# Weight sums of a seven-product scheme formed from DRAM to DRAM by GpSimd's DMAs, and the last down products in five groups between the pairs

## Chip, core and metric

One core of one Trainium2 chip runs one program. The metric is the device time of one execution in microseconds; lower is better. The kernel before takes 2364.74 us, the median of three runs (2363.32 to 2365.43).

## What is computed

Two transformer blocks run one after the other, in 32-bit floating point. The first block has two layers over 16 meta tokens and 512 tokens, width 1024. The second block, which the change touches, has one layer over 512 tokens: a mixer of four branches, then a gated feed-forward of width 2816. Its last part is

```python
h = rms_norm(x, ffn_norm)
act = jax.nn.silu(h @ w_gate) * (h @ w_up)
x = x + act @ w_down          # w_gate, w_up: 1024 x 2816, w_down: 2816 x 1024
```

## The kernel before, in words

**Layout.** Everything is held transposed: `hT` is eight tiles of 128 features by 528 positions in SBUF. A weight tile (128 x 1024, 512 KB) holds the 128 output features of one step for all eight blocks of input features.

**Precision.** Each 32-bit matrix is split into a high part (`hi`, a cast by ScalarE, now and then by VectorE) and a low part (`lo`, a subtraction on VectorE). A product is three matmuls for each block: high by high, high by low, low by high. So each weight goes through a raw place, a high place and a low place in SBUF.

**Order of the work.** A helper class `Order` (from line 382) records every operation; `flush` (line 505) plans them at the end of each stage, with modelled costs (`cost`, line 413), delays between engines (`latency`, line 368), and a rank for each stage (`RANK`, line 362), in which the record number stands against the length of the chain of work that still follows. Stage 5 of six, `block2_mixer` (line 1336), has rank (1, 30); the last, `block2_ffn` (line 1728), has (1, 5). `flush` fixes only the order of the instructions on each engine's own queue. The engines run by themselves and wait for each other by semaphores where data or places demand it. All operations are issued by one line of a helper, L493, so the profile names that line for nearly everything, and the tiles tell the groups apart. All DMAs are issued by SyncE's queue (SP). GpSimd (POOL) sets four constants at the start and does nothing else.

**The last stage.** Output tiles f = 0 and 1 of gate and up are plain products: 24 matmuls of 512 columns each (`gate_up`, line 1843). For f = 2 to 21, gate and up are computed together as one two by two block product by seven products in place of eight (`gate_up_fast`, line 1815; called a pair here): 7 x 4 x 3 = 84 matmuls of 256 columns. It needs sums of weight blocks. `weights` (line 1801) loads two packed rows `r1` and `r2` of `w_gs2` and forms `s13` (1024 columns, one addition on VectorE) and `s24` (two additions of 512 columns), then splits `r1`, `s13`, `s24` and half of `r2` into high and low. The raw, high and low places are rings of five tiles each (line 1747): three that the whole kernel uses (`w_raw`, `w_hi`, `w_lo`) and two of this stage (`s_raw`, `s_hi`, `s_lo`).

The down product (`down`, line 1853) goes by groups of f, (0, 8), (8, 16) and (16, 22) (`GROUPS`, line 29). For each of the eight output tiles m it loads one weight tile, splits it, multiplies, and VectorE adds the result into `hT[m]`. A group's down product is recorded behind the first pair of the next group; the last one, with the stores of the output, ends the kernel. `early` (line 1750) moves the records of loads and splits ahead by 500 numbers, so that they are planned before the products they serve.

Of the kernel before, what the change touches and what calls it, by code (L numbers as in the profile page):

```python
# [11 lines left out]
F32 = mybir.dt.float32  # L12
F32R = mybir.dt.float32r
AF = mybir.ActivationFunctionType
ALU = mybir.AluOpType
AX = mybir.AxisListType
PSUM = bass.MemoryType.PSUM
DRAM = bass.MemoryType.DRAM

P = 128  # L20
D = 1024
KD = 8
# [4 lines left out]
DFF = 2816  # L27
NFT = DFF // P
GROUPS = ((0, 8), (8, 16), (16, 22))
EPS = 1e-6  # L30
NEG = -(2.0 ** 100)
FILL = -3.0e38
# [11 lines left out]
FS = 2  # L44
# [145 lines left out]
def prepare(i):  # L190
    i = {k: np.asarray(v) for k, v in i.items()}
    a = {}
    a["h0"] = np.concatenate([i["meta_tokens"], i["x"][0]], 0).T.reshape(KD, P, NR)
    a["w_even"] = pack(i["even_w_in"][0], even_tiles())
    wo = i["even_w_out"][0]
    a["w_eo_0"] = pack(wo[512:512 + RF * P], whole(0, D))
    a["w_eo_1"] = pack(np.concatenate([wo[512 + RF * P:], wo[:512]], 0), whole(0, D))
    for l in range(2):
        g, u = pack(i["ffn_w_gate"][l], whole(0, DFF)), pack(i["ffn_w_up"][l], whole(0, DFF))
        a[f"w_gu{l}"] = np.stack([g, u], 1).reshape(2 * NFT, P, D)  # L200
        for n, (f0, f1) in enumerate(GROUPS):
            a[f"w_dn{l}_{n}"] = pack(i["ffn_w_down"][l][f0 * P:f1 * P], whole(0, D))
    a["w_odd"] = pack(i["odd_w_in"][0], odd_tiles())
    oo = i["odd_w_out"][0]
    a["w_oo_0"] = pack(oo[:OSP * P], whole(0, D))
    a["w_oo_1"] = pack(oo[OSP * P:], whole(0, D))
    a["w_2"] = pack(i["w_in_2"][0], list(w2_list().values()))
    for n, k in enumerate(("w_fox_out_2", "w_conv_out_2", "w_mlstm_out_2", "w_swa_out_2")):
        a[f"w_br{n}"] = pack(i[k][0], whole(0, D))
    a["w_mg"] = pack(i["w_merge_out_2"][0], whole(0, D))  # L210
    g, u = pack(i["w_gate_2"][0], whole(0, DFF)), pack(i["w_up_2"][0], whole(0, DFF))
    a["w_gu2"] = np.stack([g[:FS], u[:FS]], 1).reshape(2 * FS, P, D)
    a["w_gs2"] = paired(g[FS:], u[FS:]).reshape(-1, P, D)
    for n, (f0, f1) in enumerate(GROUPS):
        a[f"w_dn2_{n}"] = pack(i["w_down_2"][0][f0 * P:f1 * P], whole(0, D))
    g = [col(i["norm_mix"][0]), col(i["norm_ffn"][0]), col(i["norm_mix"][1]), col(i["norm_ffn"][1]),
         col(i["norm_final"]), col(i["attn_norm_2"][0]), col(i["ffn_norm_2"][0]), col(i["even_gn_gain"][0])]
    a["gains"] = np.concatenate(g, 1)
    cw = [np.concatenate([col(i["ffn_conv_w"][l][t]) for t in range(3)] + [col(i["ffn_conv_b"][l])], 1) for l in range(2)]
    a["convp"] = np.concatenate(cw, 1)  # L220
    two = lambda v: np.concatenate([v, v])[:, None]
    a["hgain"] = np.concatenate([two(i["fox_q_gain_2"][0]), two(i["fox_k_gain_2"][0]), two(i["swa_q_gain_2"][0]),
                                 two(i["swa_k_gain_2"][0]), col(i["mlstm_h_gain_2"][0])]
                                + [col(i["conv_w_2"][0][t]) for t in range(3)], 1)
    a["hbias"] = np.stack([i["fox_f_bias_2"][0], i["mlstm_i_bias_2"][0], i["mlstm_f_bias_2"][0]], 1)
    a["sinks"] = i["swa_sinks_2"]
    a["rb1"] = i["rel_bias"]
    a["rb2"] = i["rel_bias_2"]
    a = {k: np.ascontiguousarray(v) for k, v in a.items()}
    a.update(constants())  # L230
    return a
# [134 lines left out]


def latency(a, b):
    return 2.1 if a == "SP" else LAT.get((a, b), 0.25)


class Engine:
# [9 lines left out]
class Order:  # L382
# [16 lines left out]
    def pool(self, es, name, bufs=1, space=None, side=None):  # L399
        kw = {} if space is None else {"space": space}  # L400
        if side is not None:
            kw["side"] = side
        if space is not DRAM:
            kw["reuse_waits"] = "tile"
        real = es.enter_context(self.tc.tile_pool(name=name, bufs=bufs, **kw))
        return Pool(self, real, bufs, space is PSUM, space is DRAM)
# [6 lines left out]
    def cost(self, eng, method, out, ins, k):  # L413
        n = max([self.size(out)] + [self.size(i) for i in ins if isinstance(i, View) and method in ("max", "tensor_reduce", "bn_stats")])
        if eng == "PE":
            if method == "transpose":
                return max(256, 2 * n) / 2400 + 0.003
            return (max(256, n) if ins[0].t.dt == F32R else max(512, 4 * n)) / 2400 + 0.003
        ps = any(isinstance(i, View) and i.t.pool.psum for i in ins) or out.t.pool.psum
        ptrs = sum(1 for i in ins if isinstance(i, View) and self.size(i) == 1 and n > 1)  # L420
        if eng == "ACT":
            return (0.051 if ps else 0.093) + n * 0.833e-3 + 0.093 * (ptrs + (k.get("accum_out") is not None))
        if eng == "DVE":
            c = 0.069 + 0.06 * min(ptrs, 1)
            if method == "reciprocal":
                return c + n * 6.0e-3
            if method in ("tensor_copy", "tensor_scalar") and not ps:
                return c + n * 0.521e-3
            return c + n * 1.042e-3
        if eng == "SP":  # L430
            nb = 4 * int(np.prod(out.shape))
            return max(0.1, nb / 332e3)
        return 0.1 + n * 2.2e-3

    def record(self, eng, method, a, k, also=()):
        out = a[0]
# [148 lines left out]
def body(ctx: ExitStack, tc, A, out):  # L585
# [3 lines left out]
    V, SC, G, T, DMA = O.V, O.A, O.G, O.T, O.D  # L589
    pool = lambda name, **k: O.pool(ctx, name, **k)  # L590

    def dma(o, i):
        DMA.dma_start(o, i)
# [16 lines left out]
            return (pd, pp, pd, pp, pd, pp, pp)[AllBanks.turn % 7].tile(shape, dt, name=("d", "at", "d", "at", "d", "at", "at")[AllBanks.turn % 7])  # L610

    pall = AllBanks()

    def const(name, shape, dt=F32, pl=None):
        t = (pl or cst).tile(shape, dt, name=name)
# [7 lines left out]
    for k in range(KD):  # L623
        t = res.tile([P, NR], F32, name=f"h{k}")
# [711 lines left out]
    def block2_mixer():  # L1336
        with ExitStack() as es:
# [3 lines left out]
            yp = P_("yp", bufs=1)  # L1341
            wk = P_("wk", bufs=1)
            unit = lambda name, bufs=1, p=P, dt=F32: wk.tile([p, S], dt, name=name, bufs=bufs)

            x = nxt_[0].x
            rc = rp.tile([P, 8], F32, name="rcol")
# [381 lines left out]
    def block2_ffn():  # L1728
        with ExitStack() as es:
# [20 lines left out]
            def early(fn):  # L1750
                O.shift -= 500
                v = fn()
                O.shift += 500
                return v

            def halves(raw, hi=None, lo=None):

                n = raw.shape[1]
                hi = his.tile()[:, :n] if hi is None else hi
                lo = los.tile()[:, :n] if lo is None else lo  # L1760
                SC.copy(hi, raw)
                V.tensor_tensor(lo, raw, hi.bitcast(F32), op=ALU.subtract)
                return v2(hi, P), v2(lo, P)

            def load(name, i, n=D):
                raw = raws.tile()[:, :n]
                dma(raw, A[name][i])
                return raw


# [30 lines left out]
            def weights(f):  # L1801


                r1, r2 = load("w_gs2", 2 * (f - FS)), load("w_gs2", 2 * (f - FS) + 1)
                s13, s24 = raws.tile(), raws.tile()
                two = lambda t: t.rearrange("p (a b) -> p a b", a=2)
                V.tensor_tensor(two(s13), two(r2)[:, 0:1, :].to_broadcast([P, 2, 512]), two(r1), op=ALU.add)
                V.tensor_tensor(s24[:, :512], s13[:, :512], r1[:, 512:], op=ALU.add)
                V.tensor_tensor(s24[:, 512:], s24[:, :512], r2[:, 512:], op=ALU.add)
                w1, w24, w13 = halves(r1), halves(s24), halves(s13)  # L1810
                a12 = halves(r2[:, 512:], *(fp.tile([P, 512], F32R, name=n, bufs=2) for n in ("s_hi2", "s_lo2")))
                part = lambda w, i: tuple(v[:, 4 * i:4 * i + 4, :] for v in w)
                return part(w1, 1), a12, part(w1, 0), part(w13, 0), part(w24, 0), part(w13, 1), part(w24, 1)

# [35 lines left out]
                proj(pall, wtile("w_gu2", 2 * f + 1), x, times(g, g), ONE)  # L1850
                acts[f] = split_new(g, fp, "ah", "al", 10, S)

            def down(gi):
                f0, f1 = GROUPS[gi]
                n = (f1 - f0) * P
                a = [acts[f][0] for f in range(f0, f1)], [acts[f][1] for f in range(f0, f1)]
                for m in range(KD):
                    w = early(lambda: halves(load(f"w_dn2_{gi}", m, n)))
                    proj(pall, w, a, add_h(m, NM), ONE)
                    if gi == 2:  # L1860
                        dma(out[P * m:P * m + P, :], hT[m][:, NM:])

            for gi, (f0, f1) in enumerate(GROUPS):
                for f in range(f0, f1):
                    gate_up(f)
                    if gi and f == f0:
                        down(gi - 1)
            down(2)
            O.flush()

    steps = [even_mixer, lambda: ffn(0, 1), odd_mixer, lambda: ffn(1, 3), block2_mixer, block2_ffn]
# [16 lines left out]
```

## Time and profile before

| | |
|---|---|
| median of three runs | 2364.74 us (2363.32 to 2365.43) |
| the profiled execution, its own time | 2365.07 us |
| its span, first to last instruction | 2362.9 us |
| mean granted TensorE clock | 0.998 |
| busy: TensorE (PE), its weight loads (PEld) | 2334.1 us (99%), 2125.5 us (90%) |
| busy: VectorE (DVE), ScalarE (ACT), GpSimd (POOL) | 1793.0 us (76%), 968.3 us (41%), 0.2 us |
| DMA moved | 205.98 MB, mean 87 GB/s |

Matmuls are pipelined, so the busy time of one overlaps that of the next and a busy PE is not one at its peak. Waits are put down to the instruction that ended them. In the table of stretches the columns are the stretch and its length, then busy time and number of instructions of each engine, the granted clock of TensorE as a share of full speed, the mean busy share of the 16 DMA engines, and the GB/s moved.

### The profile page before, as it was taken

The numbers are of one execution on the slowest core, as the hardware profiler recorded it, in microseconds if no ns is written. First come the engines' busy times: TensorE is split into PE (matmuls) and PEld (weight loads), VectorE is DVE, ScalarE is ACT, GpSimd is POOL, SyncE is SP. The second block draws the span as 40 slices with busy tenths as digits, with TensorE's granted clock in tenths as the row PEclk, the third lists the DMA queues.
The fourth block names the chain that finished last, engine by engine and source line by source line (L and its number), as shares of the span: only waits on it lengthen the run. The fifth ranks groups of instructions, "written<-read, shape, count | busy, mean of one in ns | idle before, by whom it ended". The sixth has DMA issues, their size and how long they took to land.

```text
span 2362.9 us, 38568 instructions
## 1 busy us (share of the span) xinstructions
PE 2334.1 (99%) x15488; PEld 2125.5 (90%) x15488; DVE 1793.0 (76%) x3512; ACT 968.3 (41%) x1842; POOL 0.2 (0%) x4
## 2 busy tenths in 40 slices
PE   7999999999999999999999999999999999999999
PEld 7999999999999999999888888877888888889998
DVE  6999898764655779997665647876898877987965
ACT  4423556310111278885211203344677613443422
POOL 0000000000000000000000000000000000000000
PEclk9999999999999999999999999999999999999999
DMA  5222221322222211103223223322222122332322
GB/s 200 70 72 70 73 84 57 111 92 90 90 90 88 93 64 55 55 25 102 90 90 100 90 90 97 122 70 86 82 90 72 53 95 89 102 122 80 126 77 84
DMA packets 66546, 205.98 MB, mean 87 GB/s; under 512 B 7972, under 2 KB 14576, under 8 KB 66368
## 3 DMA queue, kind: packets, MB, share of 16 engines
q1 hardware_dynamic: 66368, 203.53, 27.1%
q8 instruction: 121, 1.98, 0.4%
q14 instruction: 57, 0.47, 0.1%
HBM read 201.37 MB, written 6.84 MB: 88 GB/s over the span
## 4 chain that ended last, share of the span: by engine, by line
PE 94%; DVE 3%; DMA 2%; issue 1%; ACT 1%; SPq 0%; DVEq 0%; ACTq 0%
PE d L493 54%; PE at L493 37%; PE pv L493 2%; DMA w_raw<-w_even 1%; DVE w_lo L493 1%; DVE s_lo L493 1%; DVE w_raw L493 0%; DMA w_raw<-w_gs 0%; DVE g L493 0%; DMA h<-h 0%; ACT w_hi L493 0%; DMA ob<-c_oh 0%; DVE sqh L493 0%; DVE s_raw L493 0%; SPq L493 0%
## 5 line engine op out<-in xcount | busy, mean ns | idle before, releaser
L493 PE MATMUL d<-xh,w_hi 128*128 128x264 f32 (+5 forms) x2082 | 616.2, 318 | 8.1 <-ACT w_hi L493 8.0
L493 PE MATMUL d<-xl,w_hi 128*128 128x264 f32 (+5 forms) x2082 | 618.4, 319 | 1.1 <-DVE xl L493 1.0
L493 PE MATMUL d<-xh,w_lo 128*128 128x264 f32 (+5 forms) x2082 | 614.0, 318 | 0.0
L493 DVE TENSOR_TENSOR w_lo<-w_raw,w_hi 128x1024 fp32r<-128x1024 f32 (+4 forms) x363 | 401.1, 1107 | 53.2 <-PE d L493 18.4
L493 PEld LDWEIGHTS d<-xh,w_hi 128*128 128x128 f32 x2082 | 377.4, 189 | 36.3 <-ACT w_hi L493 8.0
L493 PEld LDWEIGHTS d<-xl,w_hi 128*128 128x128 f32 x2082 | 377.3, 189 | 25.9 <-DVE xl L493 2.3
L493 PEld LDWEIGHTS d<-xh,w_lo 128*128 128x128 f32 x2082 | 376.3, 189 | 26.6 <-issue 1.9
L493 ACT CAST w_hi<-w_raw 128x1024 fp32r<-128x1024 f32 (+5 forms) x181 | 172.8, 955 | 328.2 <-PE d L493 230.5
L493 DVE CAST w_hi<-w_raw 128x1024 fp32r<-128x1024 f32 (+4 forms) x182 | 116.4, 640 | 188.0 <-PE d L493 113.0
L493 PE MATMUL at<-xh,w_hi 128*128 128x264 f32 (+3 forms) x822 | 240.1, 302 | 1.2 <-DVE h L493 1.2
L493 PE MATMUL at<-xh,w_lo 128*128 128x264 f32 (+3 forms) x822 | 240.1, 302 | 0.0
L493 PE MATMUL at<-xl,w_hi 128*128 128x264 f32 (+3 forms) x822 | 240.1, 302 | 0.0
L493 ACT ACTIVATE y<-g,cp 128x528 f32<-128x528 f32 (+1 forms) x44 | 36.2, 824 | 345.6 <-DVE g L493 345.6
L493 PEld LDWEIGHTS at<-xh,w_hi 128*128 128x128 f32 x822 | 152.8, 189 | 7.5 <-issue 1.6
L493 PEld LDWEIGHTS at<-xh,w_lo 128*128 128x128 f32 x822 | 152.8, 189 | 5.4
L493 PEld LDWEIGHTS at<-xl,w_hi 128*128 128x128 f32 x822 | 152.6, 189 | 5.2
L493 PE MATMUL at<-ah,w_lo 128*128 128x264 f32 (+1 forms) x350 | 113.0, 331 | 0.0
L493 PE MATMUL at<-ah,w_hi 128*128 128x264 f32 (+1 forms) x350 | 113.0, 332 | 0.0
L493 PE MATMUL at<-al,w_hi 128*128 128x264 f32 (+1 forms) x350 | 112.9, 332 | 0.0
L493 PE MATMUL d<-ah,w_hi 128*128 128x264 f32 (+1 forms) x274 | 91.1, 333 | 0.0
L493 PE MATMUL d<-al,w_hi 128*128 128x264 f32 (+1 forms) x274 | 91.0, 332 | 0.0
L493 PE MATMUL d<-ah,w_lo 128*128 128x264 f32 (+1 forms) x274 | 90.7, 332 | 0.0
(604 smaller groups left out, 4849.9 us busy)
## 6 DMA issues: line engine op xcount, KB each, us to landing
w_raw<-w_gu SPq DMA_DIRECT2D x92, 512.0 KB, 3.7
w_raw<-w SPq DMA_DIRECT2D x59, 512.0 KB, 3.6
w_raw<-w_dn SPq DMA_DIRECT2D x42, 512.0 KB, 3.8
w_raw<-w_even SPq DMA_DIRECT2D x41, 512.0 KB, 3.8
w_raw<-w_gs SPq DMA_DIRECT2D x25, 512.0 KB, 3.6
w_raw<-w_odd SPq DMA_DIRECT2D x24, 512.0 KB, 3.5
w_raw<-w_dn SPq DMA_DIRECT2D x21, 384.0 KB, 3.1
s_raw<-w_gs SPq DMA_DIRECT2D x15, 512.0 KB, 3.6
```

The source lines that it names most:

```text
L493: return f(*[r(x) for x in a], **{n: r(x) for n, x in k.items()})
```

## The change

The sums `s13` and `s24` are no longer made by VectorE. At the place in the program where the mixer begins, five DMAs for each of the 20 pairs are recorded on GpSimd's queue. They copy blocks of the weights from DRAM into new DRAM tiles of the pool `far` and add other blocks to them as they are written. The last stage loads `s13` and `s24` like any weight, and only the needed half of `r2`. The down product goes in five groups, and its output tiles are spread over the pairs of the next group in place of standing behind its first pair. The planner's numbers for POOL change with it (no other operation runs there).

```diff
--- before.py
+++ after.py
@@ -27,6 +27,7 @@
 DFF = 2816
 NFT = DFF // P
 GROUPS = ((0, 8), (8, 16), (16, 22))
+GROUPS2 = ((0, 5), (5, 10), (10, 15), (15, 19), (19, 22))
 EPS = 1e-6
 NEG = -(2.0 ** 100)
 FILL = -3.0e38
@@ -211,7 +212,7 @@
     g, u = pack(i["w_gate_2"][0], whole(0, DFF)), pack(i["w_up_2"][0], whole(0, DFF))
     a["w_gu2"] = np.stack([g[:FS], u[:FS]], 1).reshape(2 * FS, P, D)
     a["w_gs2"] = paired(g[FS:], u[FS:]).reshape(-1, P, D)
-    for n, (f0, f1) in enumerate(GROUPS):
+    for n, (f0, f1) in enumerate(GROUPS2):
         a[f"w_dn2_{n}"] = pack(i["w_down_2"][0][f0 * P:f1 * P], whole(0, D))
     g = [col(i["norm_mix"][0]), col(i["norm_ffn"][0]), col(i["norm_mix"][1]), col(i["norm_ffn"][1]),
          col(i["norm_final"]), col(i["attn_norm_2"][0]), col(i["ffn_norm_2"][0]), col(i["even_gn_gain"][0])]
@@ -366,7 +367,7 @@
 
 
 def latency(a, b):
-    return 2.1 if a == "SP" else LAT.get((a, b), 0.25)
+    return 2.1 if a in ("SP", "POOL") else LAT.get((a, b), 0.25)
 
 
 class Engine:
@@ -430,7 +431,7 @@
         if eng == "SP":
             nb = 4 * int(np.prod(out.shape))
             return max(0.1, nb / 332e3)
-        return 0.1 + n * 2.2e-3
+        return 4.0
 
     def record(self, eng, method, a, k, also=()):
         out = a[0]
@@ -610,6 +611,22 @@
             return (pd, pp, pd, pp, pd, pp, pp)[AllBanks.turn % 7].tile(shape, dt, name=("d", "at", "d", "at", "d", "at", "at")[AllBanks.turn % 7])
 
     pall = AllBanks()
+    far = pool("far", bufs=1, space=DRAM)
+    block_sums = {}
+
+    def add_blocks(name, i):
+
+
+        r1, r2 = A[name][2 * i], A[name][2 * i + 1]
+        two = lambda t: t.rearrange("p (a b) -> p a b", a=2)
+        twice_ = lambda r, c0: bass.AP(tensor=r.tensor, offset=r.offset + c0, ap=[[D, P], [0, 2], [1, 512]])
+        s13, s24 = (far.tile([P, D], F32, name=f"{name}{n}{i}") for n in ("a", "b"))
+        G.dma_start(two(s13), twice_(r2, 0))
+        G.dma_start(s13, r1, accum_op=ALU.add, max_dma_last_dim=4 * D)
+        G.dma_start(two(s24), s13[:, None, :512].to_broadcast([P, 2, 512]))
+        G.dma_start(two(s24), twice_(r1, 512), accum_op=ALU.add)
+        G.dma_start(s24[:, 512:], r2[:, 512:], accum_op=ALU.add)
+        block_sums[name, i] = s13, s24
 
     def const(name, shape, dt=F32, pl=None):
         t = (pl or cst).tile(shape, dt, name=name)
@@ -1341,6 +1358,8 @@
             yp = P_("yp", bufs=1)
             wk = P_("wk", bufs=1)
             unit = lambda name, bufs=1, p=P, dt=F32: wk.tile([p, S], dt, name=name, bufs=bufs)
+            for i in range(NFT - FS):
+                add_blocks("w_gs2", i)
 
             x = nxt_[0].x
             rc = rp.tile([P, 8], F32, name="rcol")
@@ -1762,9 +1781,9 @@
                 V.tensor_tensor(lo, raw, hi.bitcast(F32), op=ALU.subtract)
                 return v2(hi, P), v2(lo, P)
 
-            def load(name, i, n=D):
-                raw = raws.tile()[:, :n]
-                dma(raw, A[name][i])
+            def load(src):
+                raw = raws.tile()[:, :src.shape[1]]
+                dma(raw, src)
                 return raw
 
 
@@ -1801,14 +1820,11 @@
             def weights(f):
 
 
-                r1, r2 = load("w_gs2", 2 * (f - FS)), load("w_gs2", 2 * (f - FS) + 1)
-                s13, s24 = raws.tile(), raws.tile()
-                two = lambda t: t.rearrange("p (a b) -> p a b", a=2)
-                V.tensor_tensor(two(s13), two(r2)[:, 0:1, :].to_broadcast([P, 2, 512]), two(r1), op=ALU.add)
-                V.tensor_tensor(s24[:, :512], s13[:, :512], r1[:, 512:], op=ALU.add)
-                V.tensor_tensor(s24[:, 512:], s24[:, :512], r2[:, 512:], op=ALU.add)
+                i = f - FS
+                r1, r2 = load(A["w_gs2"][2 * i]), load(A["w_gs2"][2 * i + 1][:, 512:])
+                s13, s24 = (load(t) for t in block_sums["w_gs2", i])
                 w1, w24, w13 = halves(r1), halves(s24), halves(s13)
-                a12 = halves(r2[:, 512:], *(fp.tile([P, 512], F32R, name=n, bufs=2) for n in ("s_hi2", "s_lo2")))
+                a12 = halves(r2, *(fp.tile([P, 512], F32R, name=n, bufs=2) for n in ("s_hi2", "s_lo2")))
                 part = lambda w, i: tuple(v[:, 4 * i:4 * i + 4, :] for v in w)
                 return part(w1, 1), a12, part(w1, 0), part(w13, 0), part(w24, 0), part(w13, 1), part(w24, 1)
 
@@ -1850,22 +1866,21 @@
                 proj(pall, wtile("w_gu2", 2 * f + 1), x, times(g, g), ONE)
                 acts[f] = split_new(g, fp, "ah", "al", 10, S)
 
-            def down(gi):
-                f0, f1 = GROUPS[gi]
-                n = (f1 - f0) * P
+            def down(gi, ms):
+                f0, f1 = GROUPS2[gi]
                 a = [acts[f][0] for f in range(f0, f1)], [acts[f][1] for f in range(f0, f1)]
-                for m in range(KD):
-                    w = early(lambda: halves(load(f"w_dn2_{gi}", m, n)))
+                for m in ms:
+                    w = early(lambda: halves(load(A[f"w_dn2_{gi}"][m])))
                     proj(pall, w, a, add_h(m, NM), ONE)
-                    if gi == 2:
+                    if gi == len(GROUPS2) - 1:
                         dma(out[P * m:P * m + P, :], hT[m][:, NM:])
 
-            for gi, (f0, f1) in enumerate(GROUPS):
+            for gi, (f0, f1) in enumerate(GROUPS2):
                 for f in range(f0, f1):
                     gate_up(f)
-                    if gi and f == f0:
-                        down(gi - 1)
-            down(2)
+                    if gi:
+                        down(gi - 1, range(KD * (f - f0) // (f1 - f0), KD * (f + 1 - f0) // (f1 - f0)))
+            down(len(GROUPS2) - 1, range(KD))
             O.flush()
 
     steps = [even_mixer, lambda: ffn(0, 1), odd_mixer, lambda: ffn(1, 3), block2_mixer, block2_ffn]
```

## Rows read from the trace of the kernel before

**Rows 1.** The table of stretches of the whole execution (columns as above):
```profile
0.00:20.00 20.00, 10.98 (x59) 9.37 (x60) 13.34 (x26) 15.61 (x24) 0.20 (x4) 1.00 0.87 293
20.00:50.00 30.00, 26.37 (x204) 24.56 (x202) 16.45 (x28) 6.16 (x12) 0.00 (x0) 1.00 0.57 195
...
60.00:300.00 240.00, 239.90 (x1835) 229.15 (x1834) 221.37 (x576) 98.15 (x188) 0.00 (x0) 1.00 0.22 71
...
600.00:1980.00 1380.00, 1377.76 (x8513) 1220.87 (x8512) 1015.35 (x1933) 590.52 (x1191) 0.00 (x0) 1.00 0.26 83
1980.00:2363.00 383.00, 370.99 (x2408) 337.06 (x2406) 297.94 (x449) 143.94 (x189) 0.00 (x0) 0.99 0.29 95
```

**Rows 2.** PE's waits, 1980 to 2363 us: who waited for whom, total us, times, longest:
```profile
PE at L493 <- DVE sp L493: 4.3, 3, 2.3
PE d L493 <- DVE sp L493: 1.5, 1, 1.5
PE d L493 <- DVE w_lo L493: 1.3, 3, 0.4
PE at L493 <- DVE s_lo L493: 0.4, 1, 0.4
PE at L493 <- DVE w_lo L493: 0.4, 1, 0.4
PE at L493 <- ACT sp L493: 0.2, 1, 0.2
```

**Rows 3.** PE's waits, 0 to 60 us:
```profile
PE d L493 <- ACT w_hi L493: 8.0, 1, 8.0
PE at L493 <- ACT ikh L493: 4.8, 1, 4.8
```

**Rows 4.** The chain that ended last, 0 to 60 us: start, us, what:
```profile
30.43 19.03 DMA w_raw<-w_even
```

**Rows 5.** Two finer stretches of the last stage:
```profile
2040.00:2100.00 60.00, 55.39 (x452) 54.12 (x452) 57.88 (x91) 27.54 (x36) 0.00 (x0) 1.00 0.37 119
2160.00:2220.00 60.00, 57.28 (x467) 56.79 (x466) 56.05 (x89) 26.07 (x36) 0.00 (x0) 0.97 0.32 106
```

**Rows 6.** DVE's groups by shape, 1980 to 2363 us: busy us, mean ns | idle before:
```profile
L493 DVE TENSOR_TENSOR w_lo<-w_raw,w_hi 128x1024 fp32r<-128x1024 f32 x32 | 39.1, 1221 | 3.1 <-ACT w_hi L493 2.7 <-PE at L493 0.2
...
L493 DVE TENSOR_TENSOR al<-g,ah 128x512 fp32r<-128x512 f32 x22 | 15.1, 686 | 1.5 <-ACT ah L493 1.4
...
L493 DVE TENSOR_TENSOR h<-at,h 128x512 f32<-128x512 f32 x16 | 11.0, 688 | 25.5 <-PE at L493 25.5
...
L493 DVE TENSOR_TENSOR w_raw<-s_raw,w_raw 128x1024 f32<-128x1024 f32 x7 | 8.5, 1218 | 0.7 <-DMA w_raw<-w_gs 0.7
L493 DVE TENSOR_TENSOR g<-sv,rrow 128x256 f32<-128x256 f32 x20 | 8.4, 419 | 0.1
L493 DVE TENSOR_TENSOR w_raw<-w_raw,w_raw 128x512 f32<-128x512 f32 x11 | 7.5, 685 | 0.1
```

**Rows 7.** The chain that ended last, 2200 to 2300 us: a pair's and a down product's pace:
```profile
2207.80 1.44 PE at L493 x12
...
2263.90 5.62 PE at L493 x24
```

**Rows 8.** A finer stretch of the start:
```profile
5.00:10.00 5.00, 2.03 (x7) 1.73 (x8) 2.57 (x4) 3.14 (x5) 0.00 (x0) 1.00 1.00 366
```

**Rows 9.** The DMA view: queue (packets, MB, share), issues (KB each, us to landing):
```profile
q1 hardware_dynamic: 66368, 203.53, 27.1%
...
w_raw<-w_gs SPq DMA_DIRECT2D x25, 512.0 KB, 3.6
...
bv<-bv SPq DMA_DIRECT2D x1, 3068.0 KB
```

**Rows 10.** POOL's last row in the timeline: start us, us, engine, what:
```profile
0.33 0.10 POOL L1881 MEMSET const-uint8-127<- 128x1 uint8 x1
```

**Rows 11.** SP's timeline, the one large DRAM to DRAM copy:
```profile
29.13 0.76 SPq L493 DMA_DIRECT2D bv<-bv  x1
```

## The prediction

> **What bounds the kernel now.** The table of stretches comes first [rows 1]. TensorE (PE) is busy 239.90 of 240 us from 60 to 300 us and 1377.76 of 1380 us from 600 to 1980 us. There no other engine's work is worth time. It is short of work in two places: the first 50 us, and the last feed-forward from 1980 us on, which is where the change saves work. The waits of PE price both. In the last stage they are 4.3 + 1.5 us for VectorE (DVE) writing `sp`, 1.3 + 0.4 + 0.4 us for a low half of a weight, and 0.2 us for ScalarE: 8.1 us in all [rows 2]. At the start PE waits 8.0 us for the first weight and 4.8 us at about 46 us for `ikh` [rows 3]. The chain puts the second of these down to a weight load that took 19.03 us, from 30.43 to 49.46 us [rows 4]. Two finer stretches show why the last stage waits: where pairs follow pairs, DVE is busy 57.88 of 60 us and PE 55.39, and from 2160 to 2220 us PE's granted clock averages 0.97 [rows 5].
>
> **Part 1, the sums leave DVE.** A pair f ≥ 2 makes one sum of 1024 columns (1.22 us) and two of 512 (0.69 us): 2.59 us, 51.8 us over 20 pairs [rows 6]. The rest of a pair on DVE is three low halves at 1.22, one half-width one at 0.69, seven 256-wide steps at 0.42 and three 512-wide ones at 0.69 [rows 6]: 9.4 us. PE needs 84 products of 256 columns at 1.44/12 = 0.12 us [rows 7]: 10.1 us. So DVE needs 12.0 us a pair before and 9.4 after: it stops setting the pace. `sp` is the step that comes late because the sums of a later pair stand ahead of it on DVE. I let its 5.8 us go and keep the other 2.3 us, which belong to the cast and the subtraction that stay. The clock that fell after such waits cost 0.03 x 60 = 1.8 us and comes back too. Gain 7.6 us; the ends are 0 (another wait takes each place) and 8.1 + 1.8 = 9.9 us.
>
> **Part 2, the sums come by load.** SP issues four loads a pair in place of two (the second now half as wide): 20 x 0.79 MB = 16 MB more in a stage that moves 95 GB/s [rows 1] of the 366 GB/s seen at full share [rows 8]. A load lands 3.6 us after its issue [rows 9], where a DVE sum took 1.22. Five raw places with four used every 10.1 us give each 12.6 us a round; less the load, the cast of about the low half's length and the low half (1.22), 6.6 us are left, more than the 2.4 us by which a load is slower. Cost nothing. If that cover were gone (SP held behind another place's low half), it would be at most 2.4 us a pair, 48 us.
>
> **Part 3, five groups.** The down products stay 22 x 8 x 3 = 528 matmuls of 5.62/24 = 0.234 us [rows 7]. The additions into `h` become 40 in place of 24: 16 x 0.69 = 11.0 us more on DVE [rows 6]. Sixteen more low halves cost what does not shrink with width: 2 x 0.69 - 1.22 = 0.16 us each, 2.6 us. DVE falls by 51.8 - 11.0 - 2.6 = 38 us, from 298 busy us in 383 [rows 1], so this is hidden under PE. The last group has three tiles: PE takes 9 x 0.234 = 2.1 us for each output tile, DVE about 0.69 + 0.55, so the end stays PE's. Spreading down products between pairs puts PE-heavy work where DVE fell behind; it works on the same 8.1 us, which part 1 has already spent. Nothing more for it.
>
> **Part 4, GpSimd's DMAs.** Twenty tiles at five DMAs are 100 issues on POOL. What holds them until the mixer? POOL's last work is a memset at 0.33 us [rows 10]. The new DMAs read kernel inputs and write DRAM tiles of their own, so none of them waits for another engine; standing late in the recorded program delays nothing on a queue that is empty. The planner takes long remaining chains first (30 times the chain's length against the record number, which runs to 100), so it issues 20 first copies, then 20 accumulations, and so on, and a step rarely waits for its own predecessor. **I expect them from about 1 us on, not during the mixer.** SP's queue is passed by nothing in its own order, but it shares the 16 DMA engines. In 5 to 10 us these are full at 366 GB/s [rows 8], and SP's transfers to 50 us are 20 x 293 + 30 x 195 GB/s = 11.7 MB [rows 1], whose last loads end PE's second wait [rows 4].
> What the copies take from SP no row shows. Least: nothing (SP's transfers go first); a gain is excluded, since added traffic brings no load earlier. Most by even sharing: SP keeps 183 GB/s, 11.7 MB take 64 us, 14 us later. The nearest row is the one large DRAM to DRAM copy, `bv`, 3068 KB (3.14 MB) issued at 29.13 us [rows 9, 11], over by 49.46 at the latest, as the loads behind it are: at least 155 GB/s. POOL drawing that leaves 211 GB/s, 11.7 MB then take 55.5 us: **6 us later**. I take it, as the only row of the same kind of transfer.
> The Trainium skill, DMA: Bandwidth & Descriptors, section "Anatomy of one DMA — SWDGE (gpsimd) path", prices a GpSimd DMA at about 2.0 us plus bytes over 436e3; for 512 KB that is an estimate of 3.2 us, 164 GB/s, by which the start would be 8 us late and the sum 2366. No row of this trace shows a GpSimd DMA.
> After 60 us the copies (about 3.5 MB a tile with the accumulations' second reads, 73 MB) run beside loads of 71 GB/s [rows 1], issued up to three weights ahead; 211 GB/s are left for them. Cost nothing; if that cover were gone, PE would starve, see below.
>
> **Sum.** The profiled execution took 2365.07 us (span 2362.9 and 2.2 outside); the median of the runs is 0.33 lower. 2365.1 - 7.6 + 6 = 2363.5; I name 2363.5 for the median too, the 0.33 being below what counts. Differences within 0.2%, 4.7 us, can't be told from none.
>
> **Rivals.**
> *The change does what it says*: the copies run beside the mixer, or the first loads are not hurt because SP's transfers are already queued from 0.7 us. For it: PE lost nothing to loads from 600 to 1980 us [rows 1]. Against it: nothing on POOL to wait for [rows 10]. It gives 2365.1 - 7.6 = 2357.5, from 2355 to 2360. Chance 0.27.
> *Slower: SP keeps only half of the DMA engines in the first 50 us.* Place: the loads ahead of PE's second wait [rows 3, 4]. Price 14 us, less 7.6: 2371.5, and 2379 if the gain at the end is nothing. It decides from a start 7.6 + 4.7 = 12.3 us late. For it: the engines are full there [rows 8]; against it: from 20 to 50 us their share is only 0.57 [rows 1], with room for a second queue. Chance 0.26.
> *Slower by far: a turn of POOL's queue moves more than one of SP's.* SP's packets average 203.53 MB / 66368 = 3.07 KB [rows 9]. If POOL's turn moves k times as much, SP keeps 366/(1 + k); below 71 GB/s, from k = 4.2 on, PE starves while copies last. At k = 8 that is 41 GB/s for some 73 MB / 325 GB/s = 225 us: 30 x 225 = 6.8 MB short, 95 us, about 2450. Nothing in this trace speaks for it. Chance 0.07.
> The same page, section "Queues, rings and completion order", states that a DMA engine turns from ring to ring by whole packets, typically 9 to 17 descriptors; with 2 KB descriptors that would be such a k. The trace has no second busy queue to test it.
> *Forecast*: both ends about cancel, 2363.5, own range 2360.5 to 2368. Chance 0.40.
>
> **How the numbers follow.** The range 2356 to 2378 takes in the first rival but its lower end, the forecast, and the slower rival but the case without gain; the starving case is outside. Faster by over 4.7 us: 0.27 of the first rival and 0.03 of the forecast's lower end, 0.30. Slower: 0.26 + 0.07, less 0.01 for a late start with the full 9.9 us back, 0.32. Within: 0.38.
>
> **What would show it.** GpSimd's DMAs in the trace's first 100 us and a DMA share near 1 there: part 4's timing right; if they stand after 1500 us, the first rival. PE's waits before 60 us at about 19 us in place of 12.8: the 6 us. In the last stage no wait for `sp`, DVE about 260 us busy, no `s_raw` or `w_raw` sums: parts 1 and 3. Waits of PE or ScalarE for `far` loads there: part 2 wrong. PE waiting for weights between 60 and 300 us: the starving case.

## The result, and the profile after

The kernel after takes **2419.71 us** (median of five runs, 2418.49 to 2421.07) against 2364.74 for the kernel before (five runs): ratio 1.0234, 95% interval 1.0219 to 1.0249. It is slower by 55 us, outside the forecast range. Its profiled execution took 2420.14 us, span 2418.0.

The table of stretches of the kernel after (columns as in [rows 1]):

```profile
0.00:20.00 20.00, 5.72 (x18) 4.32 (x18) 7.23 (x17) 8.42 (x12) 10.49 (x18) 1.00 0.92 319
20.00:50.00 30.00, 19.16 (x82) 15.77 (x83) 12.51 (x19) 10.81 (x19) 8.49 (x12) 0.88 1.05 309
50.00:120.00 70.00, 22.35 (x167) 21.72 (x166) 11.54 (x21) 5.33 (x8) 17.52 (x22) 0.65 1.01 273
60.00:300.00 240.00, 192.23 (x1443) 182.76 (x1442) 178.02 (x439) 69.53 (x125) 61.43 (x73) 0.89 0.88 217
600.00:1980.00 1380.00, 1377.77 (x8774) 1233.91 (x8773) 1001.17 (x1913) 584.16 (x1180) 0.00 (x0) 1.00 0.26 82
```

In the middle PE is busy throughout, as before. From 50 to 120 us it works 22 of 70 us while the DMA engines are full. PE's waits, 0 to 140 us, the four longest, beside [rows 3]:

```profile
PE at L494 <- ACT ikh L494: 47.6, 1, 47.6
PE d L494 <- ACT w_hi L494: 10.4, 1, 10.4
PE d L494 <- ACT xh L494: 7.1, 4, 2.9
PE d L494 <- DVE tmp L494: 6.1, 1, 6.1
```

The 4.8 us for `ikh` became 47.6. The same view from 1980 us on lists no wait at all, where [rows 2] has 8.1 us. The chain of the kernel after, 0 to 140 us, its longer DMA pieces and where PE goes on (start, us):

```profile
9.32 17.30 DMA w_raw<-c_msk
...
27.29 17.84 DMA w_raw<-w_even
...
68.63 48.77 another core or an unknown queue
...
119.13 1.64 PE at L494 x6
```

Before, PE goes on behind this wait at

```profile
51.19 1.64 PE at L493 x6
```

so it comes 67.9 us later. ScalarE's timeline names what the view of the chain calls unknown, a weight load:

```profile
117.50 1.04 ACT L494 CAST w_hi<-w_raw 128x1024 fp32r<-128x1024 f32 x1 [48.87 <-DMA w_raw<-w_even]
```

In both kernels SP issues such a load right behind the bias copy `bv` (at 30.43 us before, the load of [rows 4], and at 61.92 us after), and the cast that waits for a weight stands ahead of `ikh` on ScalarE's queue.

GpSimd's timeline, its first and last DMA issues, with the idle time before each and what ended it:

```profile
1.29 4.97 POOL L494 DMA_DIRECT2D w_gs2a<-w_gs  x7 [0.85 <-POOLq L1896]
9.78 1.64 POOL L494 DMA_DIRECT2D w_gs2a<-w_gs  x2 [3.53 <-DMA w_gs2a<-w_gs]
...
241.62 0.81 POOL L494 DMA_DIRECT2D w_gs2b<-w_gs  x1 [4.53 <-DMA w_gs2b<-w_gs]
```

The hundred DMAs are issued from 1.3 to 241.6 us. The mixer's first product, `at<-c_small,rrow`, starts at 1561.4 us in this kernel. SP's timeline has the bias copy, issued at 29.13 us before [rows 11], at

```profile
61.06 0.76 SPq L494 DMA_DIRECT2D bv<-bv  x1
```

The DMA view (as [rows 9]): SP's queue q1, GpSimd's queue q0, and GpSimd's first copies.

```profile
q1 hardware_dynamic: 74432, 219.26, 28.2%
q0 software_dynamic: 16960, 47.19, 8.4%
...
w_gs2a<-w_gs POOLq DMA_DIRECT2D x40, 512.0 KB, 21.0
```

**One mark splits the time.** The last of the small products `at<-c_small,acc` opens the norm of the last stage; the view of the tile `c_small` gives its start at the end of "first and last start". Before:

```profile
L493 PE MATMUL at<-c_small,acc x56: 247/275/275, 17.4 to 2006.1; 128*128 128x100 f32 x48, 128*16 128x100 f32 x6, 128*4 128x100 f32 x2
```

After:

```profile
L494 PE MATMUL at<-c_small,acc x56: 247/275/503, 29.3 to 2073.6; 128*128 128x100 f32 x48, 128*16 128x100 f32 x6, 128*4 128x100 f32 x2
```

The mark comes 67.5 us later; from it to the end of the span there were 356.8 us and are 344.4. So the last stage **saved 12.4 us** and the start **lost 67.5**. The mixer's first product is 67.6 us later too (1561.4 against 1493.8), and PE behind its wait for `ikh` 67.9, so next to nothing is lost or won between the start and the last stage. Of the 67.5, the bias copy is issued 31.9 us later (61.06 against 29.13), and the rest lies in the copy and behind it.

### The profile page after: what moved, and what is told of

The parts are those of the page before. It is cut to its first block, busy times and chain, and to the rows that moved or that the text cites. A ratio compares the mean times of both kernels' runs of the same rounds, so it can differ in the third digit from the quotient of the medians.

```text
span 2418.0 us, 38858 instructions
## 1 busy us (share of the span) xinstructions
PE 2338.2 (97%) x15488; PEld 2129.7 (88%) x15488; DVE 1767.3 (73%) x3496; ACT 966.8 (40%) x1846; POOL 82.6 (3%) x104
## 3 DMA queue, kind: packets, MB, share of 16 engines
q0 software_dynamic: 16960, 47.19, 8.4%
## 4 chain that ended last, share of the span: by engine, by line
PE 95%; another core or an unknown queue 2%; DMA 2%; DVE 1%; ACT 0%; issue 0%; SPq 0%; ACTq 0%; DVEq 0%
PE d L494 55%; PE at L494 38%; PE pv L494 2%; DMA w_raw<-w_even 1%; DMA w_raw<-c_msk 1%; DVE w_lo L494 0%; DVE sqh L494 0%; DVE w_hi L494 0%; ACT w_hi L494 0%; DVE h L494 0%; DVE e L494 0%; DVE acc L494 0%; DVE yo L494 0%; DVE xl L494 0%
## 5 line engine op out<-in xcount | busy, mean ns | idle before, releaser
L494 DVE TENSOR_TENSOR w_lo<-w_raw,w_hi 128x1024 fp32r<-128x1024 f32 (+5 forms) x370 | 405.0, 1096 | 70.0 <-ACT w_hi L494 32.0
L494 PE MATMUL at<-xh,w_hi 128*128 128x264 f32 (+3 forms) x802 | 233.9, 302 | 1.2 <-DVE h L494 1.2
L494 PE MATMUL at<-xh,w_lo 128*128 128x264 f32 (+3 forms) x802 | 233.9, 302 | 0.0
L494 PE MATMUL at<-xl,w_hi 128*128 128x264 f32 (+3 forms) x802 | 233.9, 302 | 0.0
```

The lines of the kernel that those rows point to most:

```text
L494: return f(*[r(x) for x in a], **{n: r(x) for n, x in k.items()})
```

## Theory, rival and experiments

**Theory:** GpSimd's copies beside the first loads make the loss; the sums that leave VectorE make the gain. **Rivals:** the five groups make the gain; the copies cost as much anywhere. In the second half the question is how the copies take 67 us: packets in turn, or the mere share of a second queue. All runs but their expectations in one table ("mark" is the start of the last `at<-c_small,acc`, "tail" the span less the mark; ratios with 95% intervals; the kernel before ran beside each group of them at 2364.2 to 2364.4):

| kernel | us, median (range) | ratio | mark | tail |
|---|---|---|---|---|
| before | 2364.74 | 1 | 2006.1 | 356.8 |
| after | 2419.71 | 1.0234 | 2073.6 | 344.4 |
| 1 copies held until the mixer | 2378.30 (2375.64 to 2379.64) | 1.0056 [1.0044, 1.0069] | 2032.1 | 344.4 |
| 2 copies held until `bv` has landed | 2352.34 (2351.77 to 2352.88) | 0.9949 [0.9936, 0.9961] | 2006.1 | 344.4 |
| 3 five groups alone | 2354.18 (2352.86 to 2354.24) | 0.9955 [0.9941, 0.9969] | 2005.1 | 347.1 |
| 4 sums alone, held as 1 | 2375.44 (2374.40 to 2377.54) | 1.0048 [1.0036, 1.0061] | 2029.7 | 343.9 |
| 5 after, `bv` by 128 rows | 2396.61 (2395.63 to 2399.86) | 1.0133 [1.0117, 1.0148] | 2052.8 | 344.3 |
| 6 before, `bv` by 128 rows | 2359.03 (2357.59 to 2361.59) | 0.9977 [0.9968, 0.9986] | 2001.7 | 356.8 |
| 7 as 1, plan of the rest as in after | 2367.31 (2364.95 to 2368.74) | 1.0010 [1.0001, 1.0019] | 2021.3 | 344.4 |
| 8 as 2, `bv` by 128 rows | 2349.19 (2347.55 to 2350.54) | 0.9933 [0.9921, 0.9946] | 2003.7 | 344.4 |
| 9 as 3, `bv` by 128 rows | 2350.80 (2348.91 to 2351.47) | 0.9940 [0.9927, 0.9954] | 2001.7 | 346.5 |
| 10 after, copies as plain rows | 2420.82 (2418.67 to 2423.02) | 1.0237 [1.0223, 1.0251] | 2076.6 | 344.4 |
| 11 as 10, rows cut to 1024 bytes | 2391.87 (2390.80 to 2393.26) | 1.0115 [1.0101, 1.0129] | 2046.7 | 344.3 |

### 1. The copies in the mixer, as the program has them

A small DMA on GpSimd's queue reads the mixer's bias table, and all copies wait for it.

```diff
             dma(t2, t1.raw(lambda t: bass.AP(tensor=t.tensor, offset=t.offset, ap=[[383, 8], [0, P], [1, 383]]), [8, P, 383]))
+            O.hold["POOL"] = G.dma_start(far.tile([8, 8], F32, name="gate"), t2[:, 0, :8])
+            for i in range(NFT - FS):
+                add_blocks("w_gs2", i)
+            O.hold = {}
```

> The changed kernel, with GpSimd's DMAs held back until the mixer's own DRAM to DRAM copy bw has landed (a small DMA that reads bw stands ahead of them on the queue). Theory: the whole loss lies in the first 120 us, because the 100 DMAs start at 1.3 us; beside the mixer they cost nothing, and the last stage keeps its saving of 12.8 us (2005.31 to 2359.92 us before, 2072.89 to 2414.75 after). So 2365 - 13 = 2352 us, and PE's wait for ikh is 4.8 us again. Rival: copies of some 240 us starve the weight loads wherever they run; then PE waits for weights in the mixer by tens of us and the time is above 2370.

Measured 2378.30, not 2352: the start's loss is gone (the wait for `ikh` is 5.0 us), but the mark is 26 us late. The mixer's first product `at<-c_small,rrow` already starts at 1503.8 us against 1493.8, before any copy: the held copies changed the plan of the other engines, which costs 10 us; 16 us are lost in the mixer. So this run mixed two things, and run 7 separates them.

### 2. The copies behind the start

The same lines stand behind the first stage's `bv` copy.

> The same, but held only until the copy bv of the first stage has landed (about 49 us), so that they run from there to about 290 us beside the first attention. Theory: as only the first 50 us and the copy bv are sensitive, this too gives 2352 us, within 3. Rival (loads starve in any stretch while the copies last): PE waits for w_hi in 50 to 300 us and the time is above 2370.

Measured 2352.34, as expected: the mark is back at 2006.1 and the whole tail is saved. The copies are issued from 48.6 to 269 us. The stretch 60 to 260 us of this kernel:

```profile
60.00:260.00 200.00, 199.90 (x1512) 189.98 (x1512) 185.37 (x473) 73.10 (x128) 67.80 (x82) 1.00 1.06 275
```

Its queues in the same stretch:

```profile
q0 software_dynamic: 14519, 41.15, 87.2%
q1 hardware_dynamic: 3865, 13.67, 18.6%
```

DMA engines at 1.06 of full and PE busy 199.90 of 200 us: SP's queue needs 13.67 MB / 200 us = 68 GB/s there and gets them. Full engines alone cost nothing in this stretch. A little later the copies cost 1.0 us: PE waits that long for VectorE's `tmp` at 267 us, a wait that the kernel before lacks, and the chain there stands on one load of 320 KB (2.7 us from issue to landing as the median of its eight in the kernel before):

```profile
251.31 10.46 DMA bt<-bv
```

### 3 and 4. Groups alone, sums alone

Run 3 is the kernel before with `GROUPS2` and its spread down products only. Run 4 is run 1 with the three old groups.

> The kernel before with the five groups set between the pairs; the sums stay on VectorE and GpSimd has no DMAs. Prediction's account: the sums on VectorE make the late sp, so the groups alone give nothing, 2362 to 2368 us. Rival: spreading the down products between the pairs already gives VectorE time to catch up; then most of the 12.8 us comes here, about 2354 us, and DVE's sums are hidden.

> The sums by DRAM as in e1_in_mixer (held until bw has landed), with the three old groups. If the sums alone remove PE's waits for sp, the time is 2355 to 2358 us (7.6 to 9.9 us saved of the 8.1 us of waits and the clock). If the groups do it, 2362 to 2366 us.

The rival of run 3 held: the groups alone shorten the tail by 9.7 us (356.8 to 347.1), the sums alone by 12.9, both by 12.4. They remove the same loss, so the gains don't add. (The expectation of run 3 gives the prediction's account as "the groups alone give nothing"; the prediction said that they work on the same 8.1 us.) PE's waits from 1980 us on in run 3:

```profile
PE at L494 <- DVE sp L494: 0.5, 1, 0.5
PE d L494 <- DVE w_lo L494: 0.4, 1, 0.4
PE at L494 <- ACT sp L494: 0.2, 1, 0.2
```

8.1 us of waits fell to 1.1 with every sum still on VectorE. Run 4 lost its gain in the mixer, as run 1 did (its mark is 23.6 us late).

### 5 and 6. The bias copy with 128 rows in its outer dimension

`bv` is written by an access of 8 heads by 128 rows by 767. The edit only turns the first two around.

```diff
-            dma(t2, t1.raw(lambda t: bass.AP(tensor=t.tensor, offset=t.offset, ap=[[767, 8], [0, P], [1, 767]]), [8, P, 767]))
+            dma(t2.rearrange("h p n -> p h n"), t1.raw(lambda t: bass.AP(tensor=t.tensor, offset=t.offset, ap=[[0, P], [767, 8], [1, 767]]), [P, 8, 767]))
```

> The changed kernel with one edit in the first stage: the copy bv is written with the 128 rows as its outer dimension in place of the 8 heads. In the changed kernel its 1024 packets of 3068 B took 48.4 us (65.6 to 114.0 us), which is 128 x (0.138 + 0.255 us), one packet of bv and one of GpSimd's in turn, if only 8 of the 16 DMA engines carry it; before, 128 x 0.132 = 16.9 us. Theory (turn by turn, and on 8 engines): on 16 engines it takes 64 x 0.393 = 25 us, PE's wait for ikh falls from 47.6 to about 24 us and the time to about 2396 us. Rival (the copy is held up by DRAM itself, or the packets' number and not the engines' decides): bv takes 48 us still and the time stays at 2420 us.

> The kernel before with the same edit to bv, and no GpSimd DMAs. Theory: bv takes 64 x 0.132 = 8.5 us in place of 16.9, so PE's wait for ikh of 4.8 us goes, and 2 to 4 us of lower clock behind it: 2356 to 2360 us. Rival: 2364 us, the wait has another cause (the order of the loads on SP's queue).

Both times came out: 2396.61 and 2359.03. In run 5 the copy is issued as late as in the kernel after (61.45 us), but the wait is

```profile
PE at L494 <- ACT ikh L494: 26.7, 1, 26.7
```

and in run 6, where [rows 3] have 4.8,

```profile
PE at L493 <- ACT ikh L493: 1.9, 1, 1.9
```

So 21 of the 67.5 us hang on the shape of this one copy. The mean busy share of the 16 DMA engines shows the eight engines directly. While `bv` runs with no load beside it, it is, before,

```profile
40.00:44.00 4.00, 4.00 (x35) 4.00 (x34) 2.84 (x5) 1.27 (x2) 0.00 (x0) 1.00 0.51 197
```

and in run 6

```profile
32.00:42.00 10.00, 10.00 (x85) 10.00 (x84) 1.66 (x4) 0.00 (x0) 0.00 (x0) 1.00 1.02 260
```

One number of run 6 missed: the copy took 14.1 us, not 8.5, since a packet took 0.190 us at this share, not the 0.132 that was expected.

### 7. The mixer again, with the plan left alone

```diff
+            n0 = O.n
...
             O.hold = {}
+            O.n = n0
```

and GpSimd's operations no longer count in the chain lengths of the others' plan.

> As e1_in_mixer, but recorded so that every other engine's order is that of the changed kernel (in e1 the hold also moved the mixer's first records, and PE lost 8.0 us to the load rb before any GpSimd DMA ran; its mixer stage was 26 us longer, 10 of them before 1504 us). Theory: loads beside the copies cost the mixer about 16 us, so 2368 us. Rival 1: all 26 us came from the moved order, 2352 us. Rival 2: the order played no part, 2378 us.

Measured 2367.31. The mixer now starts at 1492.9, and the mark is 15 us late. PE's waits of over 1 us, 1480 to 1990 us:

```profile
PE d L497 <- DVE ac L497: 8.2, 2, 7.0
PE d L497 <- DVE gt L497: 2.9, 1, 2.9
```

The kernel before has neither of them. DMA issues of the mixer, 1500 to 1750 us, in run 7:

```profile
w_raw<-w SPq DMA_DIRECT2D x30, 512.0 KB, 7.6
```

and in the kernel before:

```profile
w_raw<-w SPq DMA_DIRECT2D x31, 512.0 KB, 3.7
```

The chain of run 7 stands on two loads there, a weight and one of 128 KB:

```profile
1577.20 8.91 DMA w_raw<-w
...
1644.06 17.56 DMA sqh<-c_win
```

In the mixer a load takes twice as long to land, and where the chain needs one at once there is no slack. The 11.1 us of waits are most of the 15; behind the longest, the granted clock from 1640 to 1680 us is 0.83. What the change says it does would have brought nothing: 2367 against 2364.

### 8 and 9. The best version, and whether the sums are worth it

Run 8 is run 2 with the edit of run 5 (and run 7's change to the chain lengths); run 9 is run 3 with it, without any DMA of GpSimd's.

> e2_after_bias (GpSimd's DMAs from the landing of bv on; 2352.3 us) with bv on 16 engines. Theory: both savings add, 2352 - 5 = 2347 us. Rival: the earlier start of GpSimd's DMAs meets loads of the first 50 us and gives the saving back, 2352 us or more.

> The kernel before with the five groups alone (sums on VectorE, no DMA of GpSimd) and the bias copy on 16 engines. By the theory that groups and sums remove the same waits of the last stage, this adds the two gains measured apart: 2354.2 for the groups, 5.3 us (2359.0 against 2364.4) for the bias copy: 2349, the same as the best version with the sums (2349.2), so that the DRAM sums are worth nothing beside the groups. The rival: the sums are worth the 1.8 us by which the held kernel (2352.3) stood below the groups alone (2354.2), and this lies at 2351 or above.

2349.19 and 2350.80: both beat both kernels, and their intervals overlap widely. The sums shorten the tail by 2.1 us (346.5 to 344.4), and their copies cost 2.0 us before the mark (2003.7 against 2001.7): run 8 has the wait for `tmp` of run 2 again, 1.7 us at 263 us, and a granted clock of 0.96 from 260 to 300 us. That is about the 2 us by which it misses the expected 2347. Run 9 falls between its theory and its rival. Which of the two is faster these runs don't settle.

### 10 and 11. The size of GpSimd's packets

```diff
-        G.dma_start(two(s13), twice_(r2, 0))
-        G.dma_start(s13, r1, accum_op=ALU.add, max_dma_last_dim=4 * D)
-        G.dma_start(two(s24), s13[:, None, :512].to_broadcast([P, 2, 512]))
...
+        G.dma_start(s13, r2, max_dma_last_dim=4 * D)
+        G.dma_start(s13, r1, accum_op=ALU.add, max_dma_last_dim=4 * D)
+        G.dma_start(s24, s13, max_dma_last_dim=4 * D)
...
```

Run 11 has `D` in place of `4 * D`: 1024 bytes in place of 4096.

> The changed kernel with the five DMAs of each pair as plain row copies and accumulations of whole rows, in packets of up to 4096 bytes; the sums are then not those that the products want (the block pattern is left out), the bytes are nearly those of the changed kernel. It is the partner of the next run. By the theory (packets in turn, GpSimd's as large as 4096 bytes) it is as slow as the changed kernel: 2412 to 2428 us, wait for ikh 43 to 52 us.

> As the run before, but its rows cut into packets of 1024 bytes; bytes and order are the same. By the theory that the queues take turns packet by packet and that the size of GpSimd's packets sets what SyncE's queue loses, each of the bias copy's 128 packets waits for a shorter packet of GpSimd's, about 0.10 us in place of 0.25: the bias copy takes about 30 us in place of 48, the wait for ikh falls to 15 to 30 us, and the time to 2380 to 2400 us. The rival, that bytes or the mere presence of the second queue set it (half of the engines' time each, whatever the packets), gives the same time as the run before, within 5 us.

Both times held. The queues from 50 to 70 us in run 10 (packets, MB, share):

```profile
q0 software_dynamic: 1261, 4.59, 82.0%
q1 hardware_dynamic: 483, 1.63, 21.9%
```

in run 11:

```profile
q0 software_dynamic: 2067, 3.44, 86.3%
q1 hardware_dynamic: 524, 1.61, 26.2%
```

and run 11's wait, 50.2 us in run 10:

```profile
PE at L494 <- ACT ikh L494: 29.1, 1, 29.1
```

The same bytes in shorter packets cost 29 us less (2420.82 to 2391.87): `bv` is issued 12.5 us earlier (48.17 against 60.64) and takes 16.5 us less, 36.4 where about 30 was expected. GpSimd's queue is as full as in run 10, so it isn't its presence that sets the loss. Counted from the trace's packet records, packets of 4 bytes left out, `bv` (1024 packets of 3068 bytes) in six kernels:

```
kernel     first start to last end   own packet   GpSimd's packets meanwhile   product
before            17.1 us             0.132 us      none                128 x 0.132 = 16.9 us
after             48.6 us             0.138 us      0.259 us            128 x 0.397 = 50.8 us
run 10            52.9 us             0.148 us      0.279 us            128 x 0.427 = 54.7 us
run 11            36.4 us             0.154 us      0.143 us            128 x 0.297 = 38.0 us
run 5             27.9 us             0.145 us      0.276 us             64 x 0.421 = 26.9 us
run 6             14.1 us             0.190 us      none                 64 x 0.190 = 12.2 us
```

One formula gives all six within 2.2 us: 128 packets on each of 8 engines (64 on each of 16 in runs 5 and 6), each followed by one of GpSimd's where it has any. In run 11 the copies that don't accumulate kept packets of 4096 bytes, 769 of the 2766 here, which is why its mean is 0.143 us and not the 0.112 of a packet of 1024 bytes.

## Why the prediction was wrong, step by step

**What bounds the kernel: right.** PE is busy 1377.77 of 1380 us from 600 to 1980 us, as before, and all that changed lies in the first 120 us and the last stage.

**Part 4, when: right.** "From about 1 us on, not during the mixer": 1.29 us.

**Part 4, how much: the step that failed.** It read "6 us later", with 14 us "by even sharing" as the most; measured 67.5. Two things were wrong in it.

*The division.* It shared bandwidth out by halves or less. The queues take turns by packets instead. Those of the kernel after in 10 to 20, 20 to 30 and 30 to 50 us:

```profile
q0 software_dynamic: 723, 2.63, 69.3%
q1 hardware_dynamic: 722, 1.35, 35.6%
...
q0 software_dynamic: 559, 2.04, 78.3%
q1 hardware_dynamic: 559, 0.92, 27.1%
...
q0 software_dynamic: 989, 3.61, 69.0%
q1 hardware_dynamic: 993, 2.69, 35.7%
```

723 to 722, 559 to 559, 989 to 993: one for one as long as both queues have work. From 10 to 50 us a packet of GpSimd's carries 8.28 MB / 2271 = 3.65 KB, one of SP's 4.96 MB / 2274 = 2.18 KB (the forecast had 3.07, the mean of the whole run), and SP moves 4.96 MB / 40 us = 124 GB/s where the step left it 211. The forecast's third rival had the mechanism, a turn of GpSimd's that moves k times as much, but priced it after 60 us alone, where it decides from k = 4.2. At the start, where SP wants all there is, it decides from any k: with k = 3.65/2.18 = 1.67, 366/2.67 = 137 GB/s and 11.7 MB take 85 us, 35 us more than 50. Up to the issue of `bv` SP moves the same 3280 packets, 7.46 MB, in both kernels: 54 us at that rate, 61.06 measured, 29.13 before. In this are waits for single small copies: SP waited 10.3 us for the 24 KB of `bv<-bvr` to land, 2.0 before. Runs 10 and 11 show that the size of GpSimd's packets sets the loss.

The Trainium skill, DMA: Bandwidth & Descriptors, section "Queues, rings and completion order", says that an engine turns between rings by whole packets, typically 9 to 17 descriptors. The trace agrees with turns by packets; here a packet of GpSimd's held at most 4096 bytes, two rows of 2 KB, not 9 to 17 of them, and the packets came one for one.

*The nearest row.* GpSimd's draw was taken from `bv`, 155 GB/s at least [rows 9, 11], "the only row of the same kind of transfer"; from 10 to 50 us GpSimd drew 8.28 MB / 40 us = 207. That row was itself slow by its shape: 8 heads outermost, 8 engines, which the table of packets and the shares of 0.51 and 1.02 show. Worse, it stands on the path, with the weight load behind it: on half of the engines it has to sit through a packet of GpSimd's after each of its 128. It took 31.5 us longer (48.6 against 17.1). With the 31.9 us of its later issue that is 63.4 us. The rest of the 67.9 us by which PE goes on later is at the two ends of the copy: its first packet starts 4.5 us behind the issue (1.5 before), and PE goes on 5.0 us behind its last (3.4 before). The clock is no part of it: in both kernels PE comes out of the wait at a granted clock of 0.50, 1.2 GHz (52 to 57 us before, 119 to 124 after).

The Trainium skill has a rule that bore on this and that the prediction left out, on the same page, section "Why a DMA increments its semaphore by 16 and not by 1": the number of engines is the largest up to 16 that divides the slowest dimension of both sides of the copy. The trace agrees: 8 heads, a share of 0.51, and 17.1 us against 128 x 0.132 = 16.9.

**Part 1: right in kind, too small.** 7.6 us forecast, 9.9 at most; the tail fell by 12.4. The 2.3 us of other waits that "stay" went as well, and that gives the 9.9; a freer VectorE brings the casts and subtractions sooner, but no run shows this step alone. The rest is in PE's busy time: from the mark to the end it is 345.0 us before and 340.5 after for the same 2294 matmuls, 4.5 us less, of which the clock explains 1.8. What shortened the other 2.7 was not settled. VectorE's busy time fell by 26 us and not by 38 (271.60 in the 370.5 us to the end with the same 2408 matmuls, where [rows 1] have 297.94), which cost nothing.

**Part 2: right.** No wait for a load from 1980 us on.

**Part 3: right.** The groups work on the same waits, and beside the sums they add nothing (12.4 against 12.9). What the forecast did not price is that alone they bring 9.7 us (run 3), without one DMA on GpSimd's queue.

**"After 60 us cost nothing": right to 1 or 2 us, but only there.** Run 2 shows it for the first attention, and in the kernel after PE is busy 133.91 of 134 us from 126 to 260 us. The 73 MB of that step were too many: GpSimd's queue moved 47.19 MB. In the mixer the same copies cost 15 us (run 7), so the first rival, "the change does what it says", would not have given 2357.5 but about 2367, as far as run 7's way of holding the copies shows.

**The rival on the other side** decided from a start 12.3 us late, and that point was passed by far; its size, half of the engines, was that of bytes shared evenly.

## What to carry to other kernels

A DMA on an empty queue starts when its data is ready, wherever the program records it (here at 1.29 us): give it something to wait for, and choose a stretch whose own loads need little and are issued far ahead. Price a second queue by packets in turn, its packet size over that of the queue it meets, and look first at transfers that run on few engines. When two parts of a change aim at the same wait, try each alone: here the part without new traffic brought 9.7 of the 12.4 us.

## What was not expected of the hardware

- Two queues took turns one packet for one packet, 559 to 559 in 10 us, at 3.65 KB against 1.65; cutting accumulating packets from 4096 to 1024 bytes (mean 0.25 to 0.28 us each against 0.112, beside `bv`) took 29 us off the time.
- Turning round two dimensions of one copy of 3068 KB, by itself, made the kernel before 5.4 us faster (2364.4 to 2359.0).
- GpSimd issued seven DMAs and then waited for one to land before it issued more (3.53 us before its eighth); a copy of 512 KB landed 21.0 us after its issue, and the 47.19 MB were issued over 240 us, 197 GB/s. 512 KB at that rate are 2.7 us.
- PE was busy 199.90 of 200 us beside DMA engines that were full throughout (run 2), and one load of 320 KB that took 10.46 us then cost it 1.0.
